# Earlier query loads in the chunked attention of a macaron encoder layer

## The chip, the cores and the metric

The kernel is one launch on one core of a Trainium2 chip. The metric is device time in microseconds (us) of that launch. A profiled execution also has a span, from its first to its last recorded instruction.

## The reference, cut to what matters

One layer of a streaming encoder runs over 1024 positions of width 1024: a half-weighted SwiGLU block, a mixer with two attentions side by side, a second SwiGLU block, and RMSNorms between. The mixer projects the normed input once into ten groups of 512 columns: queries, keys and values of attention A (`qa`, `ka`, `va`), the same of attention B (`qb`, `kb`, `vb`), and four groups of gates. The change touches the loads of attention A:

```python
# A: 8 heads of width 64; a query of chunk c sees the keys of chunks c-8 .. c (chunks of 64)
sc = einsum('bqhd,bkhd->bhqk', qc, kb) * scale + bias      # bias: learned, by clipped distance
p  = softmax(where(valid, sc, NEG))
oa = einsum('bhqk,bkhd->bqhd', p, vb)
```

Everything is float32; the kernel gets that precision from pairs of high and low parts.

## The kernel before, in words

**Stages.** First SwiGLU, combined projection with attention A and then attention B woven in, the up and output products, second SwiGLU. Within a stage the order of TensorE's work is written out by hand. A helper (`Lag`) counts TensorE's modelled time and emits the follow-up work of other engines when it is due.

**The filler.** `project_all` is a generator that works through the ten column groups, eight tiles `t` of 128 rows each. One step is three 128x512 matmuls (high times high, high times low, low times high), and eight steps finish one tile, which is then evacuated (`qk_evac`, `v_evac`, `g_evac`) and stored by DMA to a DRAM scratch (`qa_d`, `ka_d`, `va_d` and so on). `steps(n)` runs n steps. Before attention A come the groups `qa`, `ka` and tile 0 of `va`; then, inside the scratch pool "sa", `steps(7 * 8)` for the seven other tiles of `va`. The evacuation of `va` (L1196 cast on ScalarE, L1197 subtraction on VectorE, L1198 store) goes through a tile `stg` of two buffers.

**Attention A.** `run_a` walks over 32 pairs of query blocks: 8 heads, and in each the pairs that begin at block b = 0, 2, 4, 6 (a block is 128 queries). In the turn of a pair, first its `prefetch` emits loads; then the string `ORDER_A` mixes six filler steps (F), the scores of this pair (S0, S1, written to `s`), the values of the pair two turns back (V, written to `o`) and the transposes of the previous pair's probabilities (T). The scores of a block are taken by VectorE with the bias (L1316), ScalarE's exponential (L1322), VectorE's reciprocal (L1325) and GpSimd's scaling (L1326). `s` has one buffer.

**The loads.** All of them are issued by SyncE's queue (SP), in the order in which they are emitted; an issue that has to wait for a buffer or for stored data holds all issues behind it.

- `PairA.load(h)`: the keys of head h (`uk`, four DMAs of 128 KB at L1217, two tiles; six buffers) and its bias (`bias`, two small memsets on GpSimd at L1578 and L1579, four DMAs of 72 KB at L1575; two buffers).
- `PairA.load_q(h, half)`: the queries of four blocks of head h (`uq`, two DMAs of 256 KB at L1230; two buffers).
- `PairA.load_v(h)`: the values of head h (`uv`, one DMA of 512 KB at L1280; three buffers).

Each does nothing when its tile has been loaded already. Head 0's keys, bias and first queries are loaded before `steps(7 * 8)`. In the turn of pair (h, 2) `prefetch` emits the keys and bias of the next head and then the second half of this head's queries, which the scores of pair (h, 4), one turn later, read. In the turn of (h, 6) it emits the next head's values and then its first queries.

Of the kernel before, what the change touches and what calls it, by code (L numbers as in the profile page):

```python
# [130 lines left out]
class Weights:  # L131
# [109 lines left out]
    def next(self):  # L241
        n, limit = self.marks.get(len(self.parts), (0, 0))
        if n and self.free:
            self.marks[len(self.parts)] = (n - 1, limit)
            slot, self.limit = self.free.popleft(), limit
            for part in "hl":
                self.lent[f"w{part}{slot}"] = slot
                self.places.append(f"w{part}{slot}")
            self.load(2)
        elif self.free:  # L250
            self.split()
# [3 lines left out]
def kernel(ctx, tc, io, out):  # L255
# [42 lines left out]
    def psum_stage(name, **tags):  # L298
        stage.close()
        pool = stage.enter_context(tc.tile_pool(name=name, bufs=1, space=PSUM, reuse_waits="tile"))  # L300
        banks.clear()
        for tag, (cols, bufs) in tags.items():
            banks[tag] = lambda tag=tag, cols=cols, bufs=bufs: pe.tile(pool, [P, cols], F32, tag, bufs)
        banks["fill"] = lambda: pe.tile(fl, [P, 512], F32, "fill", 2)
# [809 lines left out]
    def steps(n):  # L1114
        for _ in range(n):
            next(filler, None)
# [140 lines left out]
    class PairA:  # L1257
# [29 lines left out]
        def prefetch(self):  # L1287
            h, b = self.h, self.b
            self.load(h)
            self.load_q(h, b // 4)  # L1290
            self.load_v(h)
            if b == 2:
                self.load(h + 1)
            if b == 6:
                self.load_v(h + 1)
            if b % 4 == 2:
                self.load_q(h + b // 4, (b // 4 + 1) % 2)

        def score(self, i):
            sp = pools["sp"]  # L1300
# [215 lines left out]
    def run_a(pairs):  # L1516

        n, filled = len(pairs), 0
        for i in range(n + 2):
            new = pairs[i] if i < n else None  # L1520
            old = pairs[i - 1] if 1 <= i <= n else None
            if new:
                new.prefetch()
            if i == n - 2:
                for half in range(2):
                    ItemB.load(0, half)
            if i == n:
                ItemB.load_q(0, 3)
            for op in ORDER_A.split():
                if op == "F":  # L1530
                    steps(1 if i < n or filled < 4 else 0)
                    filled += i >= n
                elif op[0] == "S" and new:
                    new.score(int(op[1]))
                elif op == "V" and i >= 2:
                    pairs[i - 2].values()
                elif op[0] == "T" and old:
                    old.transpose(int(op[1]), int(op[2]))
# [45 lines left out]
    with tc.tile_pool(name="sa", bufs=1, reuse_waits="tile") as sp:  # L1584
        pools["sp"] = sp
        PairA.load(0)
        PairA.load_q(0, 0)
        steps(7 * 8)
        pe.poll(all=True)
        psum_stage("pp3", s=(1024, 1), t=(512, 3), o=(512, 1))  # L1590
        run_a([PairA(h, b) for h in range(8) for b in range(0, NT, 2)])
        pe.poll(all=True)
# [190 lines left out]
```

## Time and profile before

| what | value |
|---|---|
| median of three runs | 2212.17 us (2210.03 to 2213.1) |
| the profiled execution | 2211.59 us, span 2209.5 us |
| TensorE matmuls (PE) busy | 2139.8 us, 97% of the span |
| VectorE (DVE), ScalarE (ACT), GpSimd (POOL) busy | 1449.5, 851.0, 846.1 us |
| DMA moved | 305.66 MB, mean 138 GB/s |

PE's share is so high that the time is read from the places where PE stands still or runs at a lower clock; the share of the other engines says little by itself. Attention A lies between 833 and 1081 us of the span.

### The profile page before, as it was taken

To read this page: it belongs to the slowest core of one execution; us is meant where nothing else is said; L and a number is where in the kernel's file an instruction comes from. 1 tells how busy PE (TensorE), PEld (TensorE's weight loads), DVE (VectorE), ACT (ScalarE), POOL (GpSimd) and SP (SyncE) were. 2 spreads that over 40 slices of the span, in tenths; PEclk is the share of its full clock that TensorE was granted. 3 is DMA by queue.
4 is the path that set the end of the run, shared out by engine and by line. 5 is a ranking of instruction groups with operands and counts; after the bars stand their busy time and mean duration, and the time that the engine had idled before them with its cause. 6 is when DMAs were issued, how large, how long until landed. Compare 5 with 4: busy or idle time off the path is not lost. (4 is left out here: it accounts for less than half of the span.)

```text
span 2209.5 us, 27922 instructions
## 1 busy us (share of the span) xinstructions
PE 2139.8 (97%) x10112; PEld 1783.0 (81%) x10112; DVE 1449.5 (66%) x2021; ACT 851.0 (39%) x1483; POOL 846.1 (38%) x749
## 2 busy tenths in 40 slices
PE   7999999999998998999999999999999999999996
PEld 6788888888876887888888887788788888888885
DVE  7768666687985435775665662534766666668895
ACT  5323323244333224665555552313332332334431
POOL 3645544352762313552111110000554545426483
PEclk9999999999999999999999999999999999999998
DMA  4234333376342445756544439523132332365431
GB/s 158 77 94 135 101 115 101 123 258 202 115 150 90 132 159 170 196 150 193 169 137 136 153 115 268 193 77 118 54 103 90 105 103 91 114 231 210 152 117 77
DMA packets 267602, 305.66 MB, mean 138 GB/s; under 512 B 17456, under 2 KB 177480, under 8 KB 267464
## 3 DMA queue, kind: packets, MB, share of 16 engines
q1 hardware_dynamic: 267320, 303.35, 43.1%
q8 instruction: 80, 1.31, 0.2%
q14 instruction: 58, 0.48, 0.1%
q0 software_dynamic: 144, 0.52, 0.1%
HBM read 210.21 MB, written 94.40 MB: 138 GB/s over the span
## 5 line engine op out<-in xcount | busy, mean ns | idle before, releaser
L211 ACT CAST wh<-w 128x1024 fp32r<-128x1024 f32 (+1 forms) x228 | 201.1, 900 | 400.7 <-PE mm L90 147.8
L90 PE MATMUL fill<-wh,xTh 128*128 128x512 f32 x824 | 328.1, 405 | 0.0
L90 PE MATMUL fill<-wh,xTl 128*128 128x512 f32 x816 | 315.2, 393 | 0.0
L215 DVE TENSOR_TENSOR wl<-w,wh 128x1024 fp32r<-128x1024 f32 (+1 forms) x227 | 286.7, 1278 | 35.3 <-ACT wh L211 34.8
L90 PE MATMUL fill<-wl,xTh 128*128 128x512 f32 x752 | 296.6, 394 | 0.0
L90 PE MATMUL mm<-xTl,wh 128*128 128x512 f32 (+1 forms) x572 | 220.7, 386 | 2.4 <-DVE xTl L614 1.8
L90 PE MATMUL mm<-xTh,wh 128*128 128x512 f32 (+1 forms) x572 | 221.6, 387 | 0.2 <-ACT xTh L448 0.2
L90 PE MATMUL mm<-xTh,wl 128*128 128x512 f32 (+1 forms) x572 | 220.2, 385 | 0.0
L90 PE MATMUL mm<-S,wh 128*128 128x512 f32 x640 | 197.0, 389 | 0.0
L90 PEld LDWEIGHTS fill<-wh,xTl 128*128 128x128 f32 x816 | 154.0, 189 | 33.1
L90 PEld LDWEIGHTS fill<-wh,xTh 128*128 128x128 f32 x824 | 155.7, 189 | 27.2
L90 PEld LDWEIGHTS fill<-wl,xTh 128*128 128x128 f32 x752 | 142.7, 190 | 23.3
L455 POOL TENSOR_SCALAR rs<-ss 128x1 f32<-128x1 f32 (+1 forms) x64 | 13.1, 205 | 337.2 <-ACT xn L475 237.6
L90 PEld LDWEIGHTS mm<-S,wh 128*128 128x128 f32 x640 | 120.1, 188 | 24.9
L215 DVE TENSOR_TENSOR wl<-tw,wh 128x1024 fp32r<-128x1024 f32 x80 | 124.9, 1562 | 9.3 <-ACT wh L211 9.3
L90 PEld LDWEIGHTS mm<-xTl,wh 128*128 128x128 f32 x572 | 108.6, 190 | 24.5 <-DVE xTl L614 2.2
L90 PE MATMUL mm<-wh,xTh 128*128 128x512 f32 x376 | 126.7, 390 | 0.0
L90 PEld LDWEIGHTS mm<-xTh,wh 128*128 128x128 f32 x572 | 108.6, 190 | 21.7 <-ACT xTh L448 0.7
L90 PEld LDWEIGHTS mm<-xTh,wl 128*128 128x128 f32 x572 | 108.4, 190 | 21.4 <-POOL wl L215 0.2
L90 PE MATMUL mm<-S,wl 128*128 128x512 f32 x320 | 124.5, 389 | 0.0
L90 PE MATMUL mm<-wh,xTl 128*128 128x512 f32 x360 | 121.3, 389 | 0.0
L335 POOL TENSOR_TENSOR tw<-w,w 128x512 f32<-128x512 f32 x40 | 55.0, 1376 | 152.2 <-DVE wl L215 103.7
(254 smaller groups left out, 4851.8 us busy)
## 6 DMA issues: line engine op xcount, KB each, us to landing
w<-in_w_ffn_gu SPq DMA_DIRECT2D x88, 512.0 KB, 4.3
raw<-hq_d SPq DMA_DIRECT2D x70, 512.0 KB, 3.7
hq_d<-xn SPq DMA_DIRECT2D x98, 256.0 KB, 4.5
w<-in_w_ffn_down SPq DMA_DIRECT2D x44, 512.0 KB, 5.6
w<-in_w_in SPq DMA_DIRECT2D x40, 512.0 KB, 4.3
hq_d<-x SPq DMA_DIRECT2D x42, 256.0 KB, 4.3
x_d<-x SPq DMA_DIRECT2D x16, 512.0 KB, 3.2
uq<-qa_d SPq DMA_DIRECT2D x32, 256.0 KB, 4.5
```

Of the source, the lines that this page charges most:

```text
L90: self.nc.tensor.matmul(ps, lhs, rhs, **flags)
L211: self.nc.scalar.copy(h, w)
L215: (lo_engine or self.nc.vector).tensor_tensor(l, w, h.bitcast(F32), op=ALU.subtract)
L335: nc.gpsimd.tensor_tensor(t[:, :512], u0, g0, op=ALU.subtract)
L455: nc.gpsimd.tensor_scalar(r, ss, 1.0 / n, EPS, op0=ALU.mult, op1=ALU.add)
```

## The change

`prefetch` emits a head's second half of queries ahead of the next head's keys and bias, and the next head's first queries ahead of its values. Head 0's second half of queries and head 1's keys and bias are emitted 16 steps into the 56 steps before the attention. The load of a head's own values is skipped in the turn b = 0; it is emitted for head 0 in the turn b = 2 (the other heads' values are there already).

```diff
@@ PairA.prefetch
             self.load(h)
             self.load_q(h, b // 4)
-            self.load_v(h)
+            if b % 4 == 2:
+                self.load_q(h + b // 4, (b // 4 + 1) % 2)
+            if b > 0:
+                self.load_v(h)
             if b == 2:
                 self.load(h + 1)
             if b == 6:
                 self.load_v(h + 1)
-            if b % 4 == 2:
-                self.load_q(h + b // 4, (b // 4 + 1) % 2)
@@ before the attention
         PairA.load(0)
         PairA.load_q(0, 0)
-        steps(7 * 8)
+        steps(2 * 8)
+        PairA.load_q(0, 1)
+        PairA.load(1)
+        steps(5 * 8)
         pe.poll(all=True)
```

## Rows read from the trace of the kernel before

**Rows 1.** The page, part 1: busy us, share of the span, instructions.

```profile
PE 2139.8 (97%) x10112; PEld 1783.0 (81%) x10112; DVE 1449.5 (66%) x2021; ACT 851.0 (39%) x1483; POOL 846.1 (38%) x749
```

**Rows 2.** Waits of PE, whole span: us in total, times, longest.

```profile
PE s L90 <- DMA uq<-qa_d: 8.5, 2, 5.4
```

**Rows 3.** Timeline of PE, head 0: start, us, instruction, [idle before, releaser].

```profile
841.69 0.62 PE L90 MATMUL s<-uk,uq 128*128 128x512 f32 x2
...
850.69 1.51 PE L90 MATMUL s<-uk,uq 128*128 128x512 f32 x4 [5.40 <-DMA uq<-qa_d]
...
856.16 0.76 PE L90 MATMUL s<-uk,uq 128*128 128x384 f32 x4
```

**Rows 4.** Timeline of PE, the same scores in head 5.

```profile
996.21 0.62 PE L90 MATMUL s<-uk,uq 128*128 128x512 f32 x2
...
1002.90 1.51 PE L90 MATMUL s<-uk,uq 128*128 128x512 f32 x4 [3.08 <-DMA uq<-qa_d]
...
1007.42 0.74 PE L90 MATMUL s<-uk,uq 128*128 128x384 f32 x4
```

**Rows 5.** Timeline of PE, the same scores in head 1.

```profile
879.12 0.62 PE L90 MATMUL s<-uk,uq 128*128 128x512 f32 x2
...
882.57 0.80 PE L90 MATMUL s<-uk,uq 128*128 128x512 f32 x4
883.21 0.40 PE L90 MATMUL o<-pTh,uv 128*128 128x256 f32 x2
...
885.44 0.74 PE L90 MATMUL s<-uk,uq 128*128 128x384 f32 x4
```

**Rows 6.** Windows: us, busy us of each engine, PEclk, DMA share, GB/s.

```profile
850.70:856.80 6.10, 6.10 (x22) 5.23 (x23) 1.55 (x4) 1.84 (x4) 0.80 (x1) 0.55 0.46 110
856.80:860.00 3.20, 3.20 (x20) 2.72 (x19) 2.94 (x7) 2.31 (x6) 1.45 (x2) 1.00 0.28 84
```

**Rows 7.** Timeline of SP's queue in head 0.

```profile
839.21 0.37 SPq L1280 DMA_DIRECT2D uv<-va_d  x1
839.62 2.79 SPq L1217 DMA_DIRECT2D uk<-ka_d  x4
842.45 1.51 SPq L1575 DMA_DIRECT2D bias<-e_d  x3
...
845.40 0.30 SPq L1575 DMA_DIRECT2D bias<-e_d  x1
845.75 1.18 SPq L1230 DMA_DIRECT2D uq<-qa_d  x2
```

**Rows 8.** Waits of SP's queue from 838 to 846 us.

```profile
SPq L1280 <- DMA va_d<-stg: 2.2, 1, 2.2
SPq L1575 <- DMA uv<-va_d: 1.4, 1, 1.4
```

**Rows 9.** Timeline of SP's queue in head 5.

```profile
988.24 3.85 SPq L174 DMA_DIRECT2D w<-in_w_in  x2
992.13 3.30 SPq L1217 DMA_DIRECT2D uk<-ka_d  x4
995.53 2.02 SPq L1575 DMA_DIRECT2D bias<-e_d  x4
997.65 1.18 SPq L1230 DMA_DIRECT2D uq<-qa_d  x2
```

**Rows 10.** DMA issues from 988 to 999 us: count, KB each, us to landing.

```profile
w<-in_w_in SPq DMA_DIRECT2D x2, 512.0 KB, 6.3
```

**Rows 11.** Timeline of SP's queue before the attention.

```profile
806.02 22.06 SPq L1198 DMA_DIRECT2D va_d<-stg  x6
830.12 1.75 SPq L174 DMA_DIRECT2D w<-in_w_in  x2
```

**Rows 12.** Timeline of ACT in the same stretch.

```profile
810.72 0.59 ACT L1196 CAST stg<-fill 128x512 fp32r<-128x512 f32 x1 [5.48 <-DMA va_d<-stg]
815.54 0.59 ACT L1196 CAST stg<-fill 128x512 fp32r<-128x512 f32 x1 [4.23 <-PE fill L90]
...
826.42 0.59 ACT L1196 CAST stg<-fill 128x512 fp32r<-128x512 f32 x1 [4.85 <-PE fill L90]
827.78 1.05 ACT L211 CAST wh<-w 128x1024 fp32r<-128x1024 f32 x1 [0.77 <-PE fill L90]
```

## Prediction, made before the changed kernel was run

> **What bounds the kernel now.** I read the page first: PE is busy for 97% of the span [rows 1], so a change of loads can pay only where PE itself stands still for a load. The list of PE's waits, longest first, is the second view. In it one load alone makes PE wait for any length: the queries of attention A, twice, 8.5 us together [rows 2]. Every other wait of PE in that list is on VectorE or ScalarE and lies outside what this change touches. Third, the timeline of PE at the two places. They are the first scores of pair b = 4 in head 0 [rows 3] and in head 5 [rows 4]: just the second half of a head's queries, emitted one turn earlier behind the next head's keys and bias. Fourth, head 1, which runs the same instructions without a wait, as the measure of what the turn should take [rows 5]. Fifth, the timeline of SP's queue at both places, to see what stands ahead of the queries [rows 7 to 9], and sixth SP and ACT in the stretch before the attention, into which some loads move [rows 11, 12].
>
> **What the two waits cost.** From the second scores of pair b = 2 to the first of pair b = 4, head 1 takes 882.57 - 879.12 = 3.45 us [rows 5]. Head 0 takes 850.69 - 841.69 = 9.00, an excess of 5.55 [rows 3]. Head 5 takes 1002.90 - 996.21 = 6.69, an excess of 3.24 [rows 4].
>
> The loss does not end with the wait. From the first to the second scores of pair b = 4 head 1 takes 885.44 - 882.57 = 2.87 us [rows 5], head 0 takes 5.47 [rows 3] and head 5 takes 4.52 [rows 4]. That is 2.60 and 1.65 us more. The reason is in the windows: after the idle stretch in head 0 PE's granted clock is 0.55 until 856.8 and 1.00 again behind it, that is mostly the lower of its two levels (1.2 of 2.4 GHz) [rows 6]. 6.10 us at 0.55 lose 2.7 us, which agrees with the 2.60 of the timeline. So each wait costs itself and a slow stretch: 5.55 + 2.60 = 8.15 us in head 0, 3.24 + 1.65 = 4.89 us in head 5, 13.04 us in all.
>
> **Part one: head 0's second queries, and head 1's keys and bias, move ahead of the attention.** Today SP issues the values at 839.21, four key loads, four bias loads, and only then the queries at 845.75; PE starts on them 4.94 us later [rows 3, 7]. In the changed kernel they are issued some 16 steps into the `va` tiles, near 806.5 (an estimate: right behind the store that goes at 806.02 [rows 11]), 39 us before PE wants them. The wait of 8.15 us goes.
>
> What is added in that stretch: ten issues on SP, priced by the same loads today. Keys 2.79, queries 1.18, bias from 842.45 to 845.70, thus 3.25 with its wait: 7.2 us of SP's queue [rows 7]. Behind them in SP is the store of `va` tile 2, then one store per tile, until weights are loaded at 830.12. SP does nothing else there than six short stores in 22 us [rows 11]. Tile 2's store slips to about 813.7 at the latest. The store ahead of it, issued at 806.02, released its `stg` buffer at 810.72 [rows 11, 12], 4.7 us later; so tile 2's buffer comes free near 818.4, and ACT's cast of tile 4, due at 815.54, would be up to 2.9 us late. The next cast that needs the same buffer is due at 826.42, and ACT's first weight cast at 827.78 [rows 12]. Tile 4's own store would be issued near 820 and land near 825, before both. The tile's matmul bank waits those 2.9 us, but before the attention the filler has four banks (two `fill`, two `fill2`) and PE fills one in 5.4 us, half the distance of 815.54 to 826.42 [rows 12], so PE does not notice. I price it at nothing; were the cover gone, it would be those 2.9 us. The two memsets on GpSimd only move to an idle place.
>
> **Part two: head 0's values move from turn b = 0 to turn b = 2.** SP waits 2.2 us there today for the last store of `va` to land [rows 8], so the issue goes at 839.21 in either order, for SP has nothing else in between. What changes is when PE wants them: without the wait its first scores of pair b = 4 begin at 841.69 + 3.45 = 845.14 and the first values matmul 0.64 later as in head 1 [rows 3, 5], at 845.78. The fourth bias load waited for this very load, and went at 845.40 [rows 7, 8], so the values had landed 0.4 us before they will be wanted, and that with four key loads beside them that are no longer there. Bounds: nothing, or, if it lands 7.2 us after issue (the 6.3 of the weight loads in the rows [rows 10] and one more), 846.4, a wait of 0.6 us. I take nothing. This is what is late next, but just not late.
>
> **Part three: in every later head the queries go first.** Only head 5 waits today. There SP was held by two weight loads until 992.09; keys, bias and queries follow and the queries go at 997.65, PE starting 5.25 us later [rows 4, 9]. With queries first they go at 992.13, and by the same 5.25 us PE could start at 997.4; it wants them at 1002.90 - 3.24 = 999.66. 2.3 us to spare, so the 4.89 us go. In the other heads nothing waits and nothing is won. The keys and bias of the next head go 1.2 us later (two query issues), and are not read for three turns. The next head's values also go 1.2 us later at b = 6 and are first read two turns into that head. Both cost nothing.
>
> Against that speaks the Trainium skill, "DMA: Bandwidth & Descriptors", section "Issuing engines are not separate DMA queues": all transfers end on the same 16 DMA engines and interleave, so an earlier place saves issue time more than transfer time. Taken alone, it makes head 5's queries wait for the bytes ahead of them, which is the first rival below; the sum by it would be up to 4.89 us less. No row here shows those two loads in the new order.
>
> **Sum.** 2211.59 (the profiled execution) - 8.15 - 4.89 = 2198.55 us. The median of the runs is 0.58 above the profiled execution, so 2199.1. PE paces everything behind this stage, so what it gains there it keeps.
>
> **The rivals.**
>
> *Head 5's queries still come late.* At 992.13 two weight loads of 512 KB are under way, the second issued near 991.7, and they took 6.3 us to land [rows 9, 10], until about 998.0. If the queries move only behind them and keep half of their 4 to 5 us, they come near 1000.2, 0.5 us late; if nothing is won, all 4.89 stay. For it: the queue is shared. Against it: the four key loads, as many bytes, stood ahead too and no longer do. Time 2199.6 to 2204.0.
>
> *Head 0's values take the place of the queries.* Place: the first `o` matmul. It decides if they land after 845.78. Price 0.6 us as above, without a lower clock after so short a wait; 2199.7. If it also drew in a slow stretch of 2.60: 2202.3.
>
> *The gain is given back.* If a later stage were paced by loads and not by PE, PE would wait there for what it gained here: 2212.2, the same as before. Against it: the list of PE's waits has no wait on a weight load.
>
> *Slower.* The ten loads ahead of the attention keep SP so busy that the weight loads due at 830.12 slip, and PE waits for the filler's next columns. It begins to cost when the burst takes over 23 us (from 806.5 to 830.12), three times its 7.2, and makes the kernel slower by over 0.2% only when PE then waits 13 + 4.4 us, a burst of some 41 us: 2217 and above. Nothing in the rows is near.
>
> **How the numbers follow.** Forecast 0.72; head 5 still late 0.12; values late 0.08; given back 0.05; slower 0.03. The median of the forecast is 2199.1. 2197.0 is the spread of the runs below it (about 2 us); the upper end, 2204.0, takes in both of the next cases whole. 0.2% (4.4 us) is about what a measurement of this kernel can tell from no change. Faster by more: the first three cases, 0.92; within: 0.05; slower: 0.03.
>
> **What would show it.** In the profile after: no wait of PE on `uq`; head 0's turn from second to first scores 3.45 us long; granted clock 1.00 through 845 to 857; in ACT one `stg` cast around 818 that waits for a store; head 5 without a wait. The prediction is wrong if PE waits for `uv` near 846, if the wait in head 5 stays, or if PE's waits behind 1090 us grow by what was won.

## The result, and the profile after

The changed kernel takes 2196.8 us (median of four runs, 2195.9 to 2197.53); the kernel before takes 2211.88 us in the same comparison (four runs, 2210.03 to 2213.1). The ratio is 0.9928 with a 95% interval of 0.9916 to 0.9939: 15.1 us faster. The forecast was 2199.1 with a range of 2197.0 to 2204.0. The direction and the mechanism came as forecast; the gain is 2 us larger than forecast, and the median lies 0.2 us below the range. The profiled execution took 2197.36 us (span 2195.6), 14.2 us less than the one of before.

The first view is again the list of PE's waits over the whole span (us in total, times, longest).

```profile
PE t L95 <- DVE xTl L449: 15.0, 10, 2.7
...
PE mm L90 <- DVE xn L1675: 6.1, 1, 6.1
...
PE s L90 <- DVE m L1317: 1.2, 1, 1.2
```

The waits on `uq` [rows 2] are gone. What is left at the scores is a wait of 1.2 us on VectorE at the second scores of head 0 (1.7 us before). The timeline of PE in head 0 answers to [rows 3]:

```profile
841.33 0.62 PE L90 MATMUL s<-uk,uq 128*128 128x512 f32 x2
...
844.78 0.80 PE L90 MATMUL s<-uk,uq 128*128 128x512 f32 x4
845.42 0.40 PE L90 MATMUL o<-pTh,uv 128*128 128x256 f32 x2
...
847.65 0.74 PE L90 MATMUL s<-uk,uq 128*128 128x384 f32 x4
851.88 0.75 PE L90 MATMUL s<-uk,uq 128*128 128x256 f32 x4
```

The three distances are 3.45, 2.87 and 4.23 us, 10.55 in all; the first two are those of the undisturbed head 1 [rows 5]. Head 5 has the same [rows 4]:

```profile
987.70 0.62 PE L90 MATMUL s<-uk,uq 128*128 128x512 f32 x2
991.15 0.80 PE L90 MATMUL s<-uk,uq 128*128 128x512 f32 x4
...
994.02 0.74 PE L90 MATMUL s<-uk,uq 128*128 128x384 f32 x4
```

The granted clock stays at 1.00 through the stretch where it had been 0.55 [rows 6] (columns as there):

```profile
844.80:855.30 10.50, 10.50 (x65) 9.27 (x64) 7.37 (x17) 5.72 (x13) 6.44 (x13) 1.00 0.43 117
```

SP's queue shows where the loads went. Before the attention [rows 11], at the start of head 0 [rows 7] and in head 5 [rows 9]:

```profile
806.44 0.53 SPq L1198 DMA_DIRECT2D va_d<-stg  x1
807.02 1.43 SPq L1230 DMA_DIRECT2D uq<-qa_d  x2
808.50 2.67 SPq L1217 DMA_DIRECT2D uk<-ka_d  x4
811.21 2.54 SPq L1576 DMA_DIRECT2D bias<-e_d  x4
813.92 14.22 SPq L1198 DMA_DIRECT2D va_d<-stg  x5
830.19 1.75 SPq L174 DMA_DIRECT2D w<-in_w_in  x2
...
838.74 0.37 SPq L1280 DMA_DIRECT2D uv<-va_d  x1
...
979.72 3.85 SPq L174 DMA_DIRECT2D w<-in_w_in  x2
983.66 1.81 SPq L1230 DMA_DIRECT2D uq<-qa_d  x2
985.52 2.51 SPq L1217 DMA_DIRECT2D uk<-ka_d  x4
```

The burst of ten early loads holds SP from 807.02 to 813.75. The store of `va` tile 2 goes at 813.92, and ScalarE's cast of tile 4 waits for it, as the timeline of ACT shows in place of the cast at 815.54 [rows 12]:

```profile
817.50 0.59 ACT L1196 CAST stg<-fill 128x512 fp32r<-128x512 f32 x1 [5.67 <-DMA va_d<-stg]
821.05 0.59 ACT L1196 CAST stg<-fill 128x512 fp32r<-128x512 f32 x1 [2.96 <-PE fill L90]
```

The next cast is on time, and the weight loads go at 830.19, where they went at 830.12 before. In head 5 the queries go first, right behind the same two weight loads.

### The profile page after: what moved, and what is told of

It is laid out like the page before. It is cut to its first block, busy times and chain, and to the rows that moved or that the text cites. A ratio compares the mean times of both kernels' runs of the same rounds, so it can differ in the third digit from the quotient of the medians.

```text
span 2195.6 us, 27930 instructions
## 1 busy us (share of the span) xinstructions
PE 2135.8 (97%) x10112; PEld 1779.8 (81%) x10112; DVE 1443.1 (66%) x2021; ACT 850.3 (39%) x1483; POOL 846.4 (39%) x749
```

## The experiments

**The changed kernel again.** No edit; five rounds.

> The changed kernel once more, in five rounds beside the kernel before. My theory (the two waits on queries with their slow stretches, 13.0 us, and 0.5 us of shorter waits elsewhere that vary from run to run): faster by 13 to 14 us, about 2198 where the kernel before takes 2212. Rival (the change wins something beyond the two waits, 2 us or more in every execution): faster by 15 us or more, as the first four runs had it (15.1).

Measured: 2195.94 us (2193.4 to 2197.64) beside 2211.07 for the kernel before (nine runs), ratio 0.9929, 0.9915 to 0.9943. Again 15.1 us. The interval is 12.6 to 18.8 us, so it holds 13 as well as 15. Over all unedited executions on record, 31 of the kernel before and 13 of the changed one, the means are 2211.9 and 2196.6 us, 15.3 apart. What the difference consists of had to come from traces (below).

**One part alone: the early loads.** The two lines of loads before the attention, with `prefetch` as it was:

```diff
-        steps(7 * 8)
+        steps(2 * 8)
+        PairA.load_q(0, 1)
+        PairA.load(1)
+        steps(5 * 8)
```

> Only head 0's second queries and head 1's keys and bias are moved ahead of the attention; the order of the loads in the later turns stays as before. My theory: the wait in head 0 goes (8.1 us, of which 5.5 wait and 2.6 slow stretch), the wait of 3.1 us in head 5 stays: faster by 8 to 8.5 us. Rival (the early keys and bias also let the first scores start sooner, by the 0.4 to 0.5 us seen once): 8.6 or more, with the wait of PE for VectorE at the second scores of head 0 near 1.2 instead of 1.7.

Measured: 2202.93 us, ratio 0.9962 (0.9949 to 0.9974), 8.1 us. Head 0 takes its undisturbed 10.55 us, and head 5's wait is there, the only one on a load in the list of PE's waits in the attention:

```profile
PE s L90 <- DMA uq<-qa_d: 3.3, 1, 3.3
PE s L90 <- DVE m L1316: 1.3, 1, 1.3
```

Head 5 loses 5.1 us with its slow stretch in this trace. The wait on VectorE is near the rival's 1.2, but not by the change: from the first scores of head 0 to the second scores of b = 2 the trace shown before takes 8.5 us, and six more traces of the kernel before take 8.0 to 8.2, as the changed kernel does. The two places are independent of each other, and this part is worth what head 0 lost.

**Less of that part: only the queries early.** `PairA.load_q(0, 1)` is moved, head 1's keys and bias are not.

> Only head 0's second queries are moved ahead of the attention; head 1's keys and bias and the order in the turns stay as before. My theory: the same 8 to 8.5 us as with keys and bias moved too, since only the queries were late. Rival (keys and bias beside the values make the values late, 512 KB behind nothing but with 800 KB beside them): PE waits for values near 845.8 and the gain is 1 to 3 us less.

Measured: 2203.29 us, ratio 0.9962 (0.995 to 0.9975), 7.8 us, the same as with keys and bias. Head 0 again takes 10.55 us with no wait for values, and the wait of head 5 was 3.7 us. So only the queries were late in head 0; the early keys and bias add nothing that these runs resolve.

**The other part alone: the order.** `prefetch` as in the change, nothing ahead of the attention.

```diff
             self.load(h)
             self.load_q(h, b // 4)
-            self.load_v(h)
+            if b % 4 == 2:
+                self.load_q(h + b // 4, (b // 4 + 1) % 2)
+            if b > 0:
+                self.load_v(h)
...
-            if b % 4 == 2:
-                self.load_q(h + b // 4, (b // 4 + 1) % 2)
```

> Only the order in the turns is changed (queries ahead of the next head's keys, bias and values, head 0's values in turn b = 2); nothing is moved ahead of the attention. My theory: in head 0 the queries can go right behind the weight loads, near 837, land some 5 us later, before 845, and the values still land before 845.8; so both waits go and the time is that of the full change, faster by 13 to 14 us, and the early loads are not needed. Rival (keys and bias in front of nothing still share the DMA engines with values and queries, so one of the two is late): a wait on queries or values of 1 to 4 us stays near 845, with a slow stretch if it is long: faster by 5 to 12 us.

Measured: 2201.23 us, ratio 0.9951 (0.9938 to 0.9963), 9.8 us. The rival was right. Head 5 loses nothing, but head 0 has two short waits, in the timeline of PE:

```profile
839.70 0.62 PE L90 MATMUL s<-uk,uq 128*128 128x512 f32 x2
...
844.35 0.87 PE L90 MATMUL s<-uk,uq 128*128 128x512 f32 x4 [1.03 <-DMA uq<-qa_d]
846.44 0.66 PE L90 MATMUL o<-pTh,uv 128*128 128x256 f32 x2 [1.22 <-DMA uv<-va_d]
...
850.21 0.75 PE L90 MATMUL s<-uk,uq 128*128 128x384 f32 x4
854.45 0.75 PE L90 MATMUL s<-uk,uq 128*128 128x256 f32 x4
```

SP issued the queries at 834.91 and the values at 837.39, so the queries took 9.4 us from issue to the matmul. Two weight loads went just ahead of them, and the values, keys and bias behind:

```profile
832.97 1.89 SPq L174 DMA_DIRECT2D w<-in_w_in  x2
834.91 1.33 SPq L1230 DMA_DIRECT2D uq<-qa_d  x2
837.39 0.37 SPq L1280 DMA_DIRECT2D uv<-va_d  x1
837.81 2.51 SPq L1217 DMA_DIRECT2D uk<-ka_d  x4
```

The clock then falls as well (0.71 in the window from 844.3 to 850.2), and head 0 loses 4.65 + 5.86 + 4.24 - 10.55 = 4.2 us. Here an earlier place in the queue was not enough: some of the bytes at the start of the attention have to be moved at another time. This is where the early load of the queries earns its keep.

**Head 0's values in turn b = 0.** The change, with `self.load_v(h)` unconditional again.

> The changed kernel, but head 0's values are loaded in turn b = 0 again, as before. My theory: nothing changes, 2196, since SP issues nothing between the two places and waits for the last store of the values either way. Rival (in turn b = 0 the issue comes earlier by the time in which SP would otherwise issue something else): up to 1 us either way.

Measured: 2197.4 us (2195.8 to 2197.7), ratio 0.9932 (0.9919 to 0.9944), the same as the change within their intervals; no wait for values. This edit is worth nothing that these runs resolve, as said.

**The early loads late in the stretch.** The same burst after 48 instead of 16 of the 56 steps.

```diff
-        steps(2 * 8)
+        steps(6 * 8)
         PairA.load_q(0, 1)
         PairA.load(1)
-        steps(5 * 8)
+        steps(1 * 8)
```

> The changed kernel, but with the ten early loads emitted after 48 instead of 16 of the 56 filler steps, so that their 7.2 us on SP's queue fall just ahead of the weight loads due at 830. My theory of the cover: those weight loads slip by some 4 to 5 us, ScalarE's cast of the weights with them, and since ScalarE works in order the first exponential too; PE then waits 3 to 5 us in the first turns, with a slow stretch if it is long: 2199 to 2203, 3 to 7 us above the changed kernel. Rival (the weights have slack enough, PE does not notice): the same as the changed kernel, 2196.

Measured: 2198.47 us, ratio 0.9938 (0.9925 to 0.9952). The interval overlaps that of the changed kernel and the median lies between theory and rival, so what follows rests on the trace. The burst held SP from 821.10 to 826.93, and the weight loads were issued on time; my picture of a full queue was wrong. But ScalarE's last weight cast waited 1.57 us for such a load, VectorE came to the first scores later, and PE waited twice as long as in the changed kernel at the second scores, with the clock at 0.64 behind it. The last weight cast on ACT in this run and in the changed kernel, the timeline of PE, and the window:

```profile
833.38 1.04 ACT L211 CAST wh<-w 128x1024 fp32r<-128x1024 f32 x1 [1.57 <-DMA w<-in_w_in]
```

```profile
833.78 1.05 ACT L211 CAST wh<-w 128x1024 fp32r<-128x1024 f32 x1 [0.32 <-DMA w<-in_w_in]
```

```profile
835.94 0.68 PE L90 MATMUL s<-uk,uq 128*128 128x256 f32 x2 [2.44 <-DVE m L1317]
```

```profile
835.90:840.60 4.70, 4.66 (x14) 3.79 (x15) 0.76 (x4) 1.10 (x4) 0.85 (x2) 0.64 0.88 278
```

The first turns take 10.84 us from the first scores at 831.63 to the second scores of b = 2, where the changed kernel takes 8.0 to 8.2: 2.7 us. So the place of the burst counts, through the chain from weight load to ScalarE to VectorE. By its place in the queue the load in question was issued at 828.53, 3.1 us ahead of the first scores, as in the changed kernel (830.19); the cast followed 4.85 us later instead of 3.59. In the 8 us around that issue the DMA engines were busy for 0.99 and 0.91 of the time (two windows of 4 us from 824), in the same stretch of the changed kernel for 0.27 and 0.53. That the bytes of the early loads delayed this landing fits these numbers; no run isolates it.

**How large are the two waits?** Six more profiles of the kernel before and five more of the changed one, unedited (the first of these five is that of the repeat above).

> The kernel before, profiled once more, to see whether its two waits have the same size in every execution: so far 14 executions of it and 9 of the changed kernel differ by 15.7 us in the mean, where the one trace has 13.0 us in the two waits. Theory 1 (the waits are of the same size each time; the rest is lower clock that comes and goes at the switches of stages, in either kernel): 8.5 us of waits on queries, in head 0 and head 5 alone, 13 us with the slow stretches. Theory 2 (the first trace caught short waits): over 8.5 us of waits, or a third head that waits, or slow stretches longer than 2.6 and 1.65 us behind them, 15 us in all.

> The kernel before, profiled a third time. Theory 1: 8.5 us of waits on queries in head 0 and head 5, with 13 us for them and the slow stretches behind them. Theory 2: more than that, 15 us.

> The kernel before, profiled a fourth time. So far the lost time in head 0 was 8.1 to 8.2 us in three traces, that in head 5 4.9, 5.3 and 7.5 us. Theory 1 (head 5's wait is what varies; it hangs on when two weight loads land): head 0 again 8.1, head 5 anywhere from 4.9 to 7.5, and the two come to 13 to 16 us. Theory 2 (the gain beyond 13 us lies outside the attention): head 5 near 4.9 and slow stretches at the switches of stages that the changed kernel does not have.

> The kernel before, profiled a fifth time; the same two theories: head 0 8.1 us, head 5 4.9 to 7.5 us; or the difference at the switches of stages (near 660, 690 and 1565 us), where a stretch of lower clock costs 1.1, 1.9 and 1.6 us when it is there.

> The changed kernel, profiled a third time: nothing lost in head 0 and head 5. Theory 1: the slow stretches near 660, 690 and 1565 us are there in some executions as in the kernel before, since nothing before 806 us is changed. Theory 2: they are rarer than in the kernel before.

> The changed kernel, profiled a fourth time, for the same count: nothing lost in the two heads; slow stretches at the three switches in some executions (theory 1) or hardly ever (theory 2).

> The kernel before, a sixth profile. Near 690 us, ahead of everything that the change touches, the stretch from 680 to 720 took 39.8 to 40.7 us in all five profiles of this kernel and 37.9 or 38.1 in half of those of the changed one. Chance: this stretch is short (38) in some profiles of the kernel before too. A real difference: it is long (about 40) again.

> The changed kernel, a fifth profile, for the same question. Chance: long (40) or short (38), as two and two so far. A real difference: short.

> The kernel before, a seventh profile. Chance: the stretch from 680 to 720 is short (38 us) in at least one of this and the last one; a real difference: long (40).

> The changed kernel, a sixth profile. Chance: long or short; a real difference: short (38 us).

Measured, each from the timeline of PE: the time from the second scores of b = 2 to the first of b = 6, less the 10.55 us that it takes undisturbed.

| profile of the kernel before | us | lost in head 0 | lost in head 5 | both |
|---|---|---|---|---|
| the one shown before | 2211.59 | 8.15 | 4.89 | 13.04 |
| before_look1 | 2209.3 | 8.11 | 5.30 | 13.41 |
| before_look2 | 2214.91 | 8.18 | 7.54 | 15.72 |
| before_look3 | 2211.91 | 6.13 | 6.31 | 12.44 |
| before_look4 | 2213.07 | 8.67 | 4.87 | 13.54 |
| before_look5 | 2207.66 | 7.07 | 5.21 | 12.28 |
| before_look6 | 2209.81 | 7.61 | 7.05 | 14.66 |
| mean | 2211.2 | 7.70 | 5.88 | 13.6 |

Both losses vary, head 5's most, so theory 1 with its fixed 8.1 us in head 0 does not hold. In head 0 the wait goes with the issue of the queries, which SP holds back until the fourth bias load has gone, and that one waits for the values to land [rows 8]. Counted from the second scores of b = 2 the queries are issued 2.5 to 4.1 us later; at the two earliest issues the excess over 3.45 us is 4.5 and 4.2 us, at the two latest 5.7 and 5.6. In before_look2 PE started 6.47 us after the queries' issue at 998.50, where the shown trace has 5.25, and the clock stayed low longer:

```profile
1004.97 1.51 PE L90 MATMUL s<-uk,uq 128*128 128x512 f32 x4 [4.69 <-DMA uq<-qa_d]
...
1010.44 0.83 PE L90 MATMUL s<-uk,uq 128*128 128x384 f32 x4
```

The six profiles of the changed kernel lose nothing in either head and take 2197.2 us in the mean: 14.0 us less, of which 13.6 in the two heads.

The second theory, that slow stretches at the switches of stages come with the kernel before, falls. The stretch from 680 to 720 us, ahead of every changed instruction, takes 39.8 to 40.7 us in some executions and 37.9 to 38.1 in others. After five and four profiles it looked as if it belonged to the kernel: long in five of five before, in two of four after. Two more pairs showed it short twice in the kernel before and long twice in the changed one: long in five of seven and in four of six. The stretches near 660 and 1565 us are short in two of seven and two of seven profiles of the kernel before, and in one of six and three of six of the changed one. Near 690 us it is the clock: PE's waits there add up to 4.6 to 5.3 us in all thirteen, and the clock falls in the long ones only, here in the windows of the shown kernel before, of before_look5 and of after_look5:

```profile
694.00:700.00 6.00, 5.12 (x18) 4.14 (x19) 2.75 (x5) 1.61 (x3) 0.00 (x0) 0.72 0.59 200
694.00:700.00 6.00, 4.92 (x25) 4.03 (x24) 3.18 (x5) 1.77 (x3) 0.73 (x2) 1.00 0.68 227
694.00:700.00 6.00, 5.12 (x15) 3.89 (x14) 2.49 (x4) 1.35 (x3) 0.00 (x0) 0.50 0.67 229
```

## Where the prediction was wrong, and where it was right

**The two waits: right in place and in cause.** Both go, with their slow stretches, and each part of the change removes the part of the loss that it was said to remove. Head 0 alone gave 8.1 and 7.8 us where 8.15 was the term.

**The size: the step that failed is the term of head 5, and with it the lower end of the range.** The term was worked out from one execution as 4.89 us. It is 5.88 in the mean of seven, from 4.87 to 7.54; the trace that I had was nearly the lowest. Head 0's term, 8.15, is 7.70 in the mean. Their sum was taken as fixed, 13.04, where it is 13.6 in the mean and varies from 12.3 to 15.7. The lower end of the range, 2197.0, then took in only the spread of the runs, not that of a wait whose end is set by when loads land. Taking from each of the seven executions its own two losses gives 2195.2 to 2199.5 us, 2197.6 in the mean. The profiles of the changed kernel have 2195.9 to 2199.2, 2197.2 in the mean, and the median measured, 2196.8, lies well inside.

The mis-sized terms are not the whole of it. They make 0.5 of the 2.3 us by which the median lies below 2199.1, and the mean sum of 13.6 leaves 1.7 of the 15.3 us between all executions. The two heads account for all but 0.4 us where both were read in the same profiles; whether the rest of the 1.7 is more than the spread of executions, and where it would lie, is open.

**Costs priced at nothing: right.** The cast of tile 4 was said to be up to 2.9 us late; it was 1.9 us late (817.50 against 815.54 [rows 12] and 0.07 by which the whole stretch lies later), the next one on time, and PE did not notice. The burst was priced at 7.2 us of SP's queue and took 6.7. The values of head 0 were issued at 838.74 and landed 4.6 us later, 2.1 us before they were wanted at 845.42, where the prediction had 0.4; with them in turn b = 0 the time is the same.

**The margin in head 5: right in sign, too large.** I gave the queries 2.3 us to spare by the 5.25 us of the old order. In the new order the first was issued at 983.66 and the last at 984.88, and that one landed 5.6 us later (in the list of DMA issues), near 990.5, 0.65 us ahead of the scores at 991.15. Two things that the sum left out took the rest. SP waited 0.9 us for PE to be done with the buffer of the queries (in the list of SP's waits), so the second issue went 1.2 us behind the first instead of 0.6; and it took 5.6 us to land where it took 4.5 before. In the six profiles of the changed kernel the margin is 0.5 to 1.3 us. The rival of a shared queue was closer than its chance of 0.12 says. One of its numbers was misread: the 6.3 us of [rows 10] come from the stretch of 992 to 999 us and are the median of a weight load ahead of the queries (issued at 991.71, 5.5 us) and one behind them (issued at 998.94, 7.2 us). The one ahead landed near 997.2, not 998.0.

In head 0, without the early loads, the shared queue did decide (the run with the order alone). Counted from the first scores, the queries were issued 9.1 us earlier than before, and PE started on them only 4.6 us earlier. The Trainium skill ("DMA: Bandwidth & Descriptors", "Issuing engines are not separate DMA queues") says that DMAs run on the same 16 DMA engines and interleave there, whichever engine started them. The trace agrees: issued at 834.91 among other loads, the queries needed 9.4 us until the matmul, where they had needed 4.94 [rows 3, 7]. That an earlier place saves issue time more than transfer time was my inference; in head 5 the earlier place was enough.

**The slower rival.** The burst did not fill the queue even when moved to the end of the stretch. It cost 2.7 us in that trace all the same, by another way than the one that I had named: through PE's wait on VectorE at the second scores of head 0 (1.7 us in the trace before, 2.44 there). The prediction had put every wait of PE other than those on the queries outside what the change touches; this one is not.

## What to carry to other kernels

When an engine that is the bound waits for a load, count the wait and the slow stretch behind it, and look at what the issuing queue puts ahead of that load; here two waits of 8.5 us together cost 13. Putting the load first was enough in head 5. Where more loads crowd one place, as at the start of head 0, reordering left a shorter wait on the same load and made one on the next, and issuing one of them in a quieter stretch removed both; put it well ahead of the next load that something waits for. A wait that ends with a landing has no fixed size: take it from several executions, or widen the range by what the same kind of load varies.

## What the runs showed of the hardware that was not expected

- Two waits of 1.03 and 1.22 us, two microseconds apart, and one of 2.44 us, were followed by a lower granted clock (0.71 and 0.64 in the windows above). Single waits of 1.67 and 1.20 us at the second scores of head 0, in the kernels before and after, were not: the clock is 1.00 in the 3 us behind them. I had assumed no lower clock after a wait of 0.6 us, and that was not tried.
- The same instructions take 38 or 40 us at one switch of stages in different executions of one kernel, with the same waits and another clock.
- The last 34 us of the span took 34.40 to 34.44 us in all seven profiles of the kernel before and 34.03 to 34.09 in all six of the changed one. The difference of 0.35 us lies behind the landing of the last store, in the closing instructions of the program (1.54 us from there to the end before, 1.18 after). It does not come from the waits that went: order_only, early_q_only and burst_late, in which one wait or both are gone, have 34.4 to 34.5; early_only, in which one is left, and values_first have 34.1. What in the program sets it is open.
